# First feed-forward's way down in seven block products instead of eight, its weight sums on VectorE and one by an accumulating transfer; the second feed-forward's weight sums made later

## The chip, the cores and the metric

The kernel runs on one core of a Trainium2 chip. The metric is the device time of one execution in microseconds, first to last instruction with what lies around them; lower is better. Three executions of the kernel before took 1136.99, 1137.66 and 1139.56 us, median 1137.66.

## The reference, cut to what matters

One decoder layer runs on 576 token columns (512 of a prompt, 64 of samples) of 1024 channels. Two of its five sub-layers are feed-forwards of width 2816, called f1 and f2 below:

```
def swiglu(x, w_gate, w_up, w_down):
    return (jax.nn.silu(x @ w_gate) * (x @ w_up)) @ w_down
...
    x = x + 0.5 * swiglu(rmsnorm(x, p['ffn1_norm']), p['ffn1_w_gate'], p['ffn1_w_up'], p['ffn1_w_down'])
    h = rmsnorm(x, p['mix_norm'])
    proj = h @ p['w_in']
    ...
    x = x + jnp.concatenate([y_lru, y_pool], axis=-1) @ p['w_out']
    x = x + cross_attend(rmsnorm(x, p['xattn_norm']), mem_k, mem_v, p['xattn_wq'], p['xattn_wo'])
    x = x + 0.5 * swiglu(rmsnorm(x, p['ffn2_norm']), p['ffn2_w_gate'], p['ffn2_w_up'], p['ffn2_w_down'])
```

All values are float32. The way up of a feed-forward is `x @ w_gate` and `x @ w_up`; the way down is the last product with `w_down`.

## The kernel before, in words

Channels lie on the 128 partitions, tokens along the free axis, in two halves of 288 columns (`HT`). A float32 product is made of three fp32r products: every operand is split into a high part (a cast on ScalarE, tags ending in `h`) and a low part (a subtraction on VectorE, tags ending in `l`) by `split`, and high x high, high x low and low x high are summed in PSUM. One such trio on one 128x128 weight block and 288 columns is three matmuls; all large products are of this kind.

The 2816 hidden rows are 22 chunks of 128. The first 3 chunks of f1 (2 of f2) are plain products (`std`). For the rest, gate and up of a chunk form a 2x2 block matrix (gate/up by even/odd input channels) times a 2x2 block of the input (even/odd channels by token halves). `product` computes it with seven block products of 12 matmuls, named 11, E, F, G, 12, H and 22, where plain ones would be eight. The input's sums are made once; the weights' sums must be made for each chunk, and each weight block or sum is split. PSUM tiles of a chunk are `pu`, `pc` and `pa`. In program order a chunk f is 11, E, 22 of the chunk before, F, G, 12, H. After each of the seven stands one call of `fill()`, which takes steps of the way down from the queue `steps`, so that TensorE has work while VectorE and ScalarE prepare.

f2 (flag `fast`) also makes its way down in seven block products for 16 of its 22 chunks: hidden chunks 2p and 2p+1 are a pair, whose sums `build_a` and `build_b` make (tiles `ph`, `pl`); four chunks are a group g, and `quick(g)` puts 4 quads of output (one for two of the 8 output rows) of 6 steps each on the queue, 7 x 6 matmuls per quad. The weights of a quad are fetched into `td` (one buffer) and `t2`, and `ensure` sums and splits them into `dh`, `dl` (three buffers). The results go from PSUM through ScalarE (`take`) and an accumulating transfer on GpSimd's queue into `x`. The remaining six chunks are plain (`PLAIN`, `down`, PSUM tile `pd`).

f1 makes its whole way down plain: `down` over groups of 4, 4, 4, 5 and 5 chunks, 8 output rows each, 6 matmuls per chunk and row, spread by `fill` over the chunks. Its gate/up sums are three additions in VectorE (`prepare_a`) and one (`prepare_b`) on loaded blocks `r0`, `r1`.

Two of the weight sums of f2 (per gate/up chunk, and per quad of its way down) are made far ahead, in DRAM: `background` issues on GpSimd's queue a copy of weight blocks into the scratch tensors `gsum` and `dsum`, and two jobs later a transfer that adds a block to them. There are 36 jobs (20 and 16). Before, `background` is called in f1's chunks (29 times) and at the 12 input projections of the mixer (`proj`).

The order on TensorE within a feed-forward is the program's (`mm` chains the matmuls). On the other engines a scheduler sets the order when the kernel is built; each engine then runs its own list strictly in order. Weights pass through a ring of four 512 KB buffers (tag `wr`), loaded on SyncE's queue.

Of the kernel before, what the change touches and what calls it, by code (L numbers as in the profile page):

```python
# [16 lines left out]
P = 128  # L17
DC = 8
# [4 lines left out]
FGS = (4, 4, 4, 5, 5)  # L23
# [46 lines left out]
def hybrid_step(ctx, tc, a):  # L70
# [45 lines left out]
    neg = const.tile([P, 4 * DC], F32, name="neg")  # L116
    v.tensor_scalar(neg, cst[:, :4 * DC], -1.0, None, op0=ALU.mult)

    def ncol(name, i=0):
        c = _C[name] + i  # L120
        return neg[:, c:c + 1]


    s.activation(const.tile([P, 1], F32, name="table"), ones, AF.Silu)
# [248 lines left out]
    def ffn(name, n, fp, turn, plain, head=False, fast=False):  # L373
# [3 lines left out]
        wstd, wgu, wd = a[f"{name}_s"], a[f"{name}_gu"], a[f"{name}_d" + "p" * fast]  # L377
# [7 lines left out]
        def small_tile(nm_):  # L385
            return fp.tile([P, HT], F32, tag="pc", bufs=2 if fast else 3, name=nm_)

        def full_tile(nm_):
            return fp.tile([P, T], F32, tag="e", bufs=3 if fast else 2, name=nm_)
# [30 lines left out]
        def std_out(i, pg, pu):  # L420
# [4 lines left out]
            v.tensor_mul(e, e, half)  # L425
            for p, q in pieces(pu, e):
                v.scalar_tensor_tensor(out=q, in0=p, scalar=-1.0, in1=q, op0=ALU.mult, op1=ALU.mult)
            if fast:
                raw[i] = e
            else:  # L430
                split(hh[0][:, i, :], hl[0][:, i, :], e)
# [3 lines left out]

        def load(f):
            if f < FFC:
                raws[f] = [raw_tile(f"r{i}") for i in range(2)]
                for i in range(2):
                    nc.sync.dma_start(raws[f][i], wgu[f - plain, :, 2 * i:2 * i + 2])  # L440
# [6 lines left out]
        def prepare_a(f):  # L447
            if f >= FFC:
                return
            r0, r1 = raws[f]  # L450
            (w22, w11), (w12, w21) = ([t[:, i] for i in range(2)] for t in (r0, r1))
            w = W[f] = {}
            w["22"], w["11"] = parts_of(r0, "a")
            v.tensor_add(w22, w22, w21)
            v.tensor_add(w21, w21, w11)
            v.tensor_add(w11, w11, w22)  # L456
            w["E"], w["F"] = parts_of(r0, "e")

        def prepare_b(f):
            if f >= FFC:  # L460
                return
            r0, r1 = raws.pop(f)
            w = W[f]
            one = [fp.tile([P, KP, P], F32R, tag=tag, name=f"{tag}_b") for tag in ("oh", "ol")]
            split(*one, r1[:, 0])
            w["12"] = lambda q, k: one[q][:, k, :]
            v.tensor_add(r1[:, 0], r1[:, 0], r0[:, 1])  # L467
            w["G"], w["H"] = parts_of(r1, "g")


        def load_pairs(f):
            if f < FFC:
                w, e = wgu[f - plain], gsum[f - plain].rearrange("p b (k n) -> p b k n", n=P)
                raws[f] = [raw_tile(f"r{i}") for i in range(2)]
                for (i, b), src in zip(((0, 0), (0, 1), (1, 0), (1, 1)), (e[:, 0], w[:, 1], w[:, 2], e[:, 1])):
                    nc.sync.dma_start(raws[f][i][:, b], src)

        def load_22(f):
            if f < FFC:
                raw22[f] = wp.tile([P, KP, P], F32, tag="wr", bufs=WRB, name="r22")  # L480
                nc.sync.dma_start(raw22[f], wgu[f - plain, :, 0])
# [27 lines left out]
        groups = PLAIN if fast else [(sum(FGS[:i]), FGS[i]) for i in range(len(FGS))]  # L509
        panels = [(gi, j) for gi in range(len(groups)) for j in range(DC)]  # L510
        fetched, wdown = {}, {}

        def fetch(i):

            if i < len(panels) and i not in fetched:
                gi, j = panels[i]
                c0, fg = groups[gi]
                c0 -= PLAIN[0][0] * fast
# [16 lines left out]
        def down(gi, after=None):  # L535
# [4 lines left out]
            def step(j, k):  # L540
# [12 lines left out]
                elif k == fg - 1:  # L553
                    v.tensor_add(halves(x[:, j, :]), pd[j][:, :, :HT], halves(x[:, j, :]))
                    if after:
                        after(j)
# [1065 lines left out]
```

## Time and profile before

| | |
|---|---|
| runs | 1136.99, 1137.66, 1139.56 us |
| profiled execution | 1138.62 us, span 1136.7 us |
| mean granted TensorE clock | 0.996 |
| f1's seven-product chunks and its way down | about 50.8 to 401.8 us of the span |
| mixer, attention | about 401.8 to 742 us |
| f2 and the final norm | about 742 to 1136.7 us |

All times in the profile are microseconds from the start of the span unless marked ns. PE is TensorE (matmuls), PEld its weight loads, DVE VectorE, ACT ScalarE, POOL GpSimd, SP SyncE. A row of a group of instructions reads: source line, engine, operation, tiles written <- read, sizes, count, then busy time in us and mean ns of one, then the engine's idle time before them with what ended it. A row of the timeline reads: start, duration, engine, line, operation, and in brackets the idle time before it and what ended it. A row of a stretch gives the stretch's length, the busy time of each engine with its count, the granted clock, and the DMA engines' busy share and GB/s.

### The profile page before, as it was taken

How to read it: one execution, taken by the hardware profiler on the slowest of the kernel's cores; microseconds unless marked ns; L12 is line 12 of the kernel's file. 1: busy time of each engine (PE TensorE's matmuls, PEld its weight loads, DVE VectorE, ACT ScalarE, POOL GpSimd, SP SyncE). 2: the span in 40 equal slices, each digit the busy share in tenths (PEclk: the TensorE clock that was granted, in tenths of full speed). 3: DMA queues.
4: the chain of work that ended last, by engine and by line, in shares of the span. 5: the costliest groups of instructions: out<-in, count | busy, mean ns of one | idle time of the engine just before them, and what ended most of it. 6: DMA issues, size and time to landing. Idle time of an engine off the chain costs nothing.

```text
span 1136.7 us, 21329 instructions
## 1 busy us (share of the span) xinstructions
PE 1118.5 (98%) x8536; PEld 1101.0 (97%) x8536; DVE 832.0 (73%) x1387; ACT 610.9 (54%) x1052; POOL 134.4 (12%) x176
## 2 busy tenths in 40 slices
PE   8999999999999999999999999999999999999996
PEld 8999999999999999999999889999999999999996
DVE  8877778777775687986833566769878888787654
ACT  7644344344342454885622455546666666666554
POOL 0011111111111033310000000000121111212110
PEclk9999999999999999999999999999999999999998
DMA  8356766577674388642566762223675766766652
GB/s 293 117 146 152 185 167 149 140 162 188 155 182 107 103 236 191 119 141 94 174 217 215 261 229 92 66 89 93 162 176 148 182 172 160 188 167 154 148 115 84
DMA packets 82547, 179.58 MB, mean 158 GB/s; under 512 B 8272, under 2 KB 28752, under 8 KB 82320
## 3 DMA queue, kind: packets, MB, share of 16 engines
q1 hardware_dynamic: 55456, 129.66, 35.3%
q0 software_dynamic: 24064, 45.88, 22.9%
q10 hardware_dynamic: 2928, 2.67, 0.7%
q8 instruction: 67, 1.10, 0.4%
q14 instruction: 32, 0.26, 0.1%
HBM read 156.86 MB, written 34.17 MB: 168 GB/s over the span
## 4 chain that ended last, share of the span: by engine, by line
PE 91%; DVE 4%; ACT 2%; DMA 2%; issue 1%; DVEq 0%; SPq 0%; ACTq 0%
PE pu L136 23%; PE pd L136 15%; PE pc L136 11%; PE d L136 7%; PE pa L136 5%; PE q L136 5%; PE wo L136 5%; PE xo L136 5%; PE pg L136 3%; PE k L136 2%; PE v L1347 2%; PE in_l L136 2%; PE in_p L136 2%; PE o L136 1%; PE s L136 1%
## 5 line engine op out<-in xcount | busy, mean ns | idle before, releaser
L136 PE MATMUL pd<-hh,dl 128*128 128x288 f32 x352 | 75.3, 295 | 0.0
L136 PE MATMUL pd<-hh,dh 128*128 128x288 f32 x352 | 75.0, 294 | 0.0
L136 PE MATMUL pd<-hl,dh 128*128 128x288 f32 x352 | 75.0, 294 | 0.0
L178 ACT CAST wh_e<-r 128x1024 fp32r<-128x1024 f32 x39 | 41.0, 1051 | 57.1 <-DVE r L456 27.5
L136 PE MATMUL d<-ph,dh 128*128 128x288 f32 x224 | 66.8, 298 | 0.2 <-ACT add_e L659 0.2
L136 PE MATMUL d<-ph,dl 128*128 128x288 f32 x224 | 66.3, 296 | 0.0
L136 PE MATMUL d<-pl,dh 128*128 128x288 f32 x224 | 66.0, 295 | 0.0
L676 POOL DMA_DIRECT2D x<-add_e x16 | 19.3, 1204 | 380.9 <-ACT dh L178 348.6
L136 PEld LDWEIGHTS pd<-hh,dh 128*128 128x128 f32 x352 | 56.3, 188 | 0.0
L136 PEld LDWEIGHTS pd<-hh,dl 128*128 128x128 f32 x352 | 56.2, 188 | 0.0
L136 PEld LDWEIGHTS pd<-hl,dh 128*128 128x128 f32 x352 | 56.1, 188 | 0.0
L179 DVE TENSOR_TENSOR wl_e<-r,wh_e 128x1024 fp32r<-128x1024 f32 x39 | 47.7, 1222 | 11.1 <-ACT wh_e L178 11.1
L178 ACT CAST wh_g<-r 128x1024 fp32r<-128x1024 f32 x39 | 41.0, 1052 | 20.2 <-DVE r L467 14.4
L179 DVE TENSOR_TENSOR wl_g<-r,wh_g 128x1024 fp32r<-128x1024 f32 x39 | 47.7, 1222 | 5.2 <-ACT wh_g L178 4.1
L178 ACT CAST dh<-wr_d 128x512 fp32r<-128x512 f32 (+2 forms) x50 | 30.9, 619 | 34.5 <-PE pd L136 14.7
L136 PE MATMUL pu<-n1l,wh_a 128*128 128x288 f32 x152 | 44.9, 295 | 0.0
L136 PE MATMUL pu<-n1h,wl_a 128*128 128x288 f32 x152 | 44.8, 295 | 0.0
L136 PE MATMUL pu<-n1h,wh_a 128*128 128x288 f32 x152 | 44.7, 294 | 0.0
L907 ACT ACTIVATE g<-g 128x576 f32<-128x576 f32 x39 | 26.8, 686 | 32.2 <-DVE g L906 32.2
L136 PEld LDWEIGHTS d<-ph,dh 128*128 128x128 f32 x224 | 42.1, 188 | 0.8 <-ACT add_e L659 0.4
L136 PEld LDWEIGHTS d<-pl,dh 128*128 128x128 f32 x224 | 42.3, 189 | 0.0
L179 DVE TENSOR_TENSOR dl<-td,dh 128x512 fp32r<-128x512 f32 x48 | 33.1, 689 | 12.5 <-ACT dh L178 9.3
(561 smaller groups left out, 4235.3 us busy)
## 6 DMA issues: line engine op xcount, KB each, us to landing
gsum<-f_gu POOLq DMA_DIRECT2D x40, 512.0 KB, 8.6
r<-f_gu SPq DMA_DIRECT2D x38, 512.0 KB, 4.1
r<-f_gu SPq DMA_DIRECT2D x60, 256.0 KB, 4.1
x<-add POOLq DMA_DIRECT2D x40, 288.0 KB, 4.4
r<-gsum SPq DMA_DIRECT2D x40, 256.0 KB, 3.9
dsum<-f_d POOLq DMA_DIRECT2D x32, 256.0 KB, 5.7
ck<-ck SPq DMA_DIRECT2D x16, 512.0 KB, 4.4
cv<-cv SPq DMA_DIRECT2D x16, 512.0 KB, 7.2
```

The source lines that it names most:

```text
L136: i = te.matmul(*args, **kw)
L178: s.copy(hi, src)
L179: v.tensor_tensor(out=lo, in0=src, in1=f(hi), op=ALU.subtract)
L676: nc.gpsimd.dma_start(x[:, j:j + 2, HT:], t, accum_op=ALU.add)
L907: s.activation(g, g, AF.Silu, scale=-1.0)
L1347: te.matmul(ps[:, m, :HD], lhsT=lhs[:, kd, ms], rhs=w[wi][:, k, :], start=kd == 0 and i == 0, stop=kd == DC - 1 and i == 2)
```

## The change

- f1 uses the same scheme for its way down as f2: chunks 0 to 15 by `build_a`, `build_b`, `ensure` and `quick`, the last six plain.
- f1's weight sums can't be made ahead. Of the gate/up sums, `sum_eh` makes H = r0 + r0' on VectorE and E by a transfer on GpSimd's queue that adds a block from DRAM onto `r0` after H has been read; `sum_g` makes the other two on VectorE, as in f2. Of the sums of a quad of the way down, all four are made on VectorE (in f2, two of them come from `dsum`).
- f1's way down scales by 0.5 when it evicts (as f2 does), so `half` goes; the first 16 chunks and the plain group of two add into `x` by accumulating transfers, the last group of four on VectorE.
- `background` is called in f1's last five chunks, at the 8 last evictions of f1's way down, at the 12 projections of the mixer, at 6 of the 8 output projections and at the 8 of attention's output: 39 calls.
- In f1's head, the small products that spread the norm factor stand two weight blocks later (`mid`).
- In f2, `t2` is fetched with `td` and has two buffers.

```diff
         def load_pairs(f):
             if f < FFC:
-                ...
+                r0, r1 = raws[f] = [raw_tile(f"r{i}") for i in range(2)]
+                if head:
+                    nc.sync.dma_start(r0, w[:, 0:2])
+                    nc.sync.dma_start(r1[:, 0], w[:, 2])
+                else:
+                    ...
+        def sum_eh(f):
+            if f < FFC:
+                r0, r1 = raws[f]
+                v.tensor_add(r1[:, 1], r0[:, 0], r0[:, 1])
+                nc.gpsimd.dma_start(r0[:, 0], wgu[f - plain, :, 3], accum_op=ALU.add)
...
-                if k == fg - 1 and fast:
+                if k == fg - 1 and after:
+                    xj = halves(x[:, j, :])
+                    v.scalar_tensor_tensor(out=xj, in0=pd[j][:, :, :HT], scalar=0.5, in1=xj, op0=ALU.mult, op1=ALU.add)
+                    after(j)
+                    background()
+                elif k == fg - 1:
                     add = rows.tile([P, T], F32, tag="sq", name="add")
                     s.activation(halves(add), pd[j][:, :, :HT], AF.Copy, scale=0.5)
                     nc.gpsimd.dma_start(x[:, j, :], add, accum_op=ALU.add)
-                elif k == fg - 1:
-                    v.tensor_add(halves(x[:, j, :]), pd[j][:, :, :HT], halves(x[:, j, :]))
...
+                if head:
+                    nc.sync.dma_start(t[:, 0:3], wq[g, q, :, 0:3])
...
                     if k:
                         v.tensor_add(t[:, k], t[:, k], t[:, k - 1])
+                    elif head:
+                        v.tensor_add(t[:, 3], t[:, 0], t[:, 1])
+                        v.tensor_add(t[:, 0], t[:, 0], draw[i, 0])
                     split(*w, t[:, k:k + 2])
...
-        std(cols(ps1[1]), w, range(4))
+        mid = 6 if head else 4
+        std(cols(ps1[1]), w, range(mid))
...
         for f in range(plain, FFC):
             product(U, w["11"], n, N11, True)
...
             product(C, w["E"], n, T1, True)
...
             if before:
                 finish_chunk(before)
...
-                prepare_a(f + 1)
+            (sum_eh if head else prepare_e)(f + 1)
             fill()
...
             product(A, w["12"], n, N21, False)
...
+            if head:
+                prepare_e(f + 1)
...
             product(U, w["H"], n, T3, False)
...
+            if head:
+                sum_g(f + 1)
+                prepare_g(f + 1)
+                load_pairs(f + 2)
```

The first place is VectorE in f1's seven-product chunks. In the names, `wl_e`, `wl_g`, `wl_a` are low parts of weight sums of a gate/up chunk, `dl` of the way down's weights, L454 with an output `r1` in the kernel after is `sum_eh`'s addition, and `td` holds a quad's weights. Before, in a chunk of f1:

```order
L179 TENSOR_TENSOR wl_a_3662<-r0_3578,wh_a_3661 128x1024
L454 TENSOR_TENSOR r0_3578<-r0_3578,r1_3579 128x512
L455 TENSOR_TENSOR r1_3579<-r1_3579,r0_3578 128x512
L554 TENSOR_TENSOR x_66<-pd_3527,x_66 128x576
L179 TENSOR_TENSOR dl4_3634<-wr_d4_3525,dh4_3633 128x640
L456 TENSOR_TENSOR r0_3578<-r0_3578 128x512
L833 TENSOR_TENSOR g_3518<-pu_3409,g_3518 128x288
L179 TENSOR_TENSOR wl_e_3669<-r0_3578,wh_e_3668 128x1024
```

After, at the end of chunk 12 and the start of chunk 13. Between L454 and `wl_e_2872`, which reads the same `r0_2686` after the transfer has added to it, stand three instructions:

```order
L851 TENSOR_TENSOR e1_2552<-pu_2518,e1_2552 128x288
L610 TENSOR_TENSOR td9_2655<-td9_2655,t29_2657 128x256
L852 TENSOR_TENSOR g_2618<-e1_2552,g_2618 128x288
L454 TENSOR_TENSOR r1_2687<-r0_2686 128x512
L178 TENSOR_TENSOR dl90_2747<-td9_2655,dh90_2746 128x512
L178 TENSOR_TENSOR wl_22_2812<-r22_2538,wh_22_2811 128x512
L607 TENSOR_TENSOR td9_2655<-td9_2655 128x256
L178 TENSOR_TENSOR wl_e_2872<-r0_2686,wh_e_2871 128x1024
L178 TENSOR_TENSOR dl91_2784<-td9_2655,dh91_2783 128x512
```

The additions on `r0` in place have become one addition into `r1`, the transfer on another queue and two later additions; the way down's sums and splits stand among them. The second place is the same engine one chunk later: `dl102` is the last instruction on VectorE that reads `td10`, `td11` is loaded into the same single buffer, and L609 is the first that uses it.

```order
L178 TENSOR_TENSOR dl102_3052<-td10_2845,dh102_3051 128x512
L780 TENSOR_TENSOR g_2837<-pu_2698,g_2837 128x288
L470 TENSOR_TENSOR r0_2903<-r0_2903 128x512
L178 TENSOR_TENSOR dl103_3110<-t210_2847,dh103_3109 128x256
L471 TENSOR_TENSOR r0_2903<-r0_2903,r1_2904 128x512
L181 SCALAR_TENSOR_TENSOR pl6_2908<-g_2837,ph6_2907 128x576
L574 TENSOR_TENSOR g_2837<-g_2837,t2_2909 128x288
L609 TENSOR_TENSOR td11_3056<-td11_3056 128x256
```

Before, f1 had no `td`; its down weights went through the ring of four. The third place is GpSimd's queue from the end of f1 into the mixer (`u0`, `pe0` are the first buffers of the mixer's two branches; `gsum`, `dsum` are background transfers). Before:

```order
L165 DMA gsum13_110<-f2_gu 256x1x512
L168 DMA gsum14_111<-f2_gu 128x1024
L1093 MEMSET u0_4707 128x3
L1152 MEMSET pe0_4715 128x15
L1093 MEMSET u1_4780 128x3
L1094 COPY u0_4707<-st_4524 128x8x3
L1153 COPY pe0_4715<-st_4524 128x8x15
```

After:

```order
L164 DMA dsum1_119<-f2_d 256x1x256
L167 DMA dsum1_119<-f2_d 128x512
L164 DMA gsum5_103<-f2_gu 256x1x512
L167 DMA gsum6_104<-f2_gu 128x1024
L1027 MEMSET u0_5180 128x3
L1028 COPY u0_5180<-st_4997 128x8x3
L1086 MEMSET pe0_5188 128x15
L1087 COPY pe0_5188<-st_4997 128x8x15
```

Before, the last copy ahead of the mixer's first buffers is that into `gsum14`, the fifteenth of twenty; after, it is that into `gsum6`, the seventh, issued at the last eviction of f1.

More of the change, by code (lines that the diff above doesn't have):

```diff
@@ L424, in std_out @@
             s.activation(e, e, AF.Silu, scale=-1.0)
-            v.tensor_mul(e, e, half)
+            v.tensor_mul(e, e, r)
             for p, q in pieces(pu, e):
                 v.scalar_tensor_tensor(out=q, in0=p, scalar=-1.0, in1=q, op0=ALU.mult, op1=ALU.mult)
[L428 to L431, printed above, removed]
+            raw[i] = e
         raws, W = {}, {}
[L436 to L440, printed above, removed]
         def parts_of(src, nm_):
@@ L508, in ffn @@
         steps = deque()
-        groups = PLAIN if fast else [(sum(FGS[:i]), FGS[i]) for i in range(len(FGS))]
-        panels = [(gi, j) for gi in range(len(groups)) for j in range(DC)]
+        panels = [(gi, j) for gi in range(len(PLAIN)) for j in range(DC)]
         fetched, wdown = {}, {}
@@ L855, in ffn @@
             s.copy(A, U)
-            if fast:
+            if not (head and f == plain):
                 prepare_h(f)
-                load_22(f + 1)
-                if f == FFC - 5:
-                    fetch(0)
-            else:
+            load_22(f + 1)
+            if f == FFC - 5:
+                fetch(0)
+            if head and f >= FFC - 5:
                 background()
@@ L1268, in hybrid_step @@
                 mem_square(i)
+            background()
             if j == 5:
```

244 lines of the change are left out of this document (82 added, 162 removed).

## The prediction

> **What bounds the kernel now.** I read the page's busy times, the chain of work, the groups of instructions and then stretches.
>
> ```profile
> span 1136.7 us, 21329 instructions
> PE 1118.5 (98%) x8536; PEld 1101.0 (97%) x8536; DVE 832.0 (73%) x1387; ACT 610.9 (54%) x1052; POOL 134.4 (12%) x176
> PE 91%; DVE 4%; ACT 2%; DMA 2%; issue 1%; DVEq 0%; SPq 0%; ACTq 0%
> L136 PE MATMUL pd<-hh,dl 128*128 128x288 f32 x352 | 75.3, 295 | 0.0
> ```
>
> TensorE is busy for 98% of the span and carries 91% of the chain; `pd`, the plain way down, has no idle time ahead of it. So a matmul less is worth its step, as long as nothing else sets the pace. The step is read from a run of `pd` matmuls in the chain (start, us, what), and VectorE's load from stretches of f1 (first row) and of f2, which already runs the scheme that f1 gets (second); then f1's last evictions and the mixer.
>
> ```profile
> 367.56 34.38 PE pd L136 x258
> 100.00:200.00 100.00, 100.00 (x758) 100.00 (x757) 80.39 (x120) 42.34 (x65) 14.41 (x18) 1.00 0.67 163
> 800.00:900.00 100.00, 99.84 (x752) 99.47 (x751) 81.71 (x141) 66.95 (x136) 18.12 (x19) 1.00 0.69 167
> 382.00:390.00 8.00, 8.00 (x62) 8.00 (x61) 5.96 (x9) 4.17 (x7) 0.00 (x0) 1.00 0.33 98
> 414.00:422.00 8.00, 8.00 (x64) 8.00 (x63) 6.90 (x21) 2.58 (x3) 3.23 (x8) 1.00 0.96 241
> ```
>
> One matmul takes 34.38/258 = 0.133 us. At full clock TensorE has no gap in either feed-forward, and VectorE is 80 to 82% busy in both: f2's scheme fits when two of its sums per chunk and per quad come by transfer.
>
> **The removed products.** Plain, 16 chunks by 8 rows by 6 matmuls are 768; by sevenths, 16 quads of 42 are 672. 96 x 0.133 = 12.8 us off the path. Nothing else on TensorE changes in number.
>
> **The head.** The wait below is at the place where the norm's small matmuls now stand 12 matmuls (1.6 us) later.
>
> ```profile
> PE pg L136 <- DVE rf_n L272: 1.3, 1, 1.3
> ```
>
> It may go. But the order of VectorE puts `wl_e`, a sum of `td0` and one of `r0` (1.14 + 0.33 + 0.60 us by the rows below) ahead of the eviction that frees the next PSUM tile, about what is won. I take 0, between -1.3 and +1.
>
> **What VectorE gets.** From pc(8) to pc(12) of the new order, a group of four chunks, I count 12 instructions of 1024 columns, 28 of 512, 8 of 576, 38 of 288 and 20 of 256. These rows of f2 stand back to back, so that a start less the one before is the price:
>
> ```profile
> 889.94 0.41 DVE L639 TENSOR_TENSOR td<-td 128x256 f32<-128x256 f32 x1
> 890.27 0.45 DVE L915 TENSOR_TENSOR g<-e,g 128x288 f32<-128x288 f32 x1
> 890.64 1.22 DVE L179 TENSOR_TENSOR wl_e<-r,wh_e 128x1024 fp32r<-128x1024 f32 x1
> 891.78 0.45 DVE L596 TENSOR_TENSOR t<-g 128x288 f32<-128x288 f32 x1
> ...
> 893.49 0.69 DVE L492 TENSOR_TENSOR r<-r,r 128x512 f32<-128x512 f32 x1
> 894.09 0.75 DVE L179 TENSOR_TENSOR pl<-g,ph 128x576 fp32r<-128x576 f32 x1
> 894.76 0.69 DVE L179 TENSOR_TENSOR dl<-td,dh 128x512 fp32r<-128x512 f32 x1
> ...
> 896.03 0.42 DVE L639 TENSOR_TENSOR td<-td 128x256 f32<-128x256 f32 x1
> 897.14 0.69 DVE L179 TENSOR_TENSOR dl<-td,dh 128x512 fp32r<-128x512 f32 x1 [0.69 <-ACT dh L178]
> ```
>
> 256: 0.33, 288: 0.37, 512: 0.60, 576: 0.67, 1024: 1.14 us. Together 12 x 1.14 + 28 x 0.60 + 8 x 0.67 + 38 x 0.37 + 20 x 0.33 = 56.5 us. TensorE's group is 4 x 84 + 4 x 42 = 504 matmuls, 67.0 us. So 10.5 us are left for VectorE's waits, where f2 had 5.0 more (four sums of 512 and eight of 256 fewer: 2.4 + 2.6).
>
> Two kinds of wait don't shrink when VectorE is late, since each is released by VectorE itself. First, a sum, its cast on ScalarE and the subtraction: the last row waits 0.69 us so. In the order I find some six such places in a group where too little stands between, 3.5 us; f2 shows these as ScalarE's share of idle time:
>
> ```profile
> L179 DVE TENSOR_TENSOR dl<-td,dh 128x512 fp32r<-128x512 f32 x45 | 31.0, 689 | 11.8 <-ACT dh L178 8.6 <-PE pu L136 2.1
> L179 DVE TENSOR_TENSOR wl<-r,wh 128x512 fp32r<-128x512 f32 x15 | 10.3, 689 | 7.6 <-ACT wh L178 7.6
> L908 DVE TENSOR_TENSOR g<-g,rstd_n 128x576 f32<-128x576 f32 x15 | 11.4, 758 | 8.6 <-ACT g L907 8.6
> ```
>
> Those three wait for ScalarE 24.8 us in 15 chunks, 6.6 a group, much of it with time to spare. I take 4, between 2 and 6.6.
>
> Second, new waits on transfers: `sum_eh` (L454), transfer, cast, `wl_e`; and the last read of a `td`, its load, the next sum. No row shows an accumulate from DRAM into SBUF. The nearest (in the page's list of transfers, the last number is the us to landing):
>
> ```profile
> x<-add POOLq DMA_DIRECT2D x40, 288.0 KB, 4.4
> x<-add_e POOLq DMA_DIRECT2D x16, 288.0 KB, 6.4
> gsum<-f_gu POOLq DMA_DIRECT2D x40, 512.0 KB, 8.6
> r<-f_gu SPq DMA_DIRECT2D x60, 256.0 KB, 4.1
> td<-f_d SPq DMA_DIRECT2D x16, 256.0 KB, 5.0
> wr_o<-w_out SPq DMA_DIRECT2D x8, 512.0 KB, 3.6
> ```
>
> The cast takes 1.05 us:
>
> ```profile
> L178 ACT CAST wh_e<-r 128x1024 fp32r<-128x1024 f32 x15 | 15.8, 1053 | 5.4 <-PE pu L136 5.4
> ```
>
> I take 3.9 us for the accumulate: `x<-add` is nearest by queue, size and shape, and the evictions of the way down alone land from 3.5 us up (below), with f1's background gone. Ends: 3.5 and 6.4. With the cast and 0.3 for semaphores that is 5.3 us from L454's end to `wl_e`. In the order 6.7, 1.5, 8.6 and 3.9 us of VectorE's work stand between in the four chunks, so it waits 3.8 and, with the 0.7 of a cast counted above, 0.7 us. For a `td` load I take 4.2 us (384 KB in one piece; ends 3.6 and 5.0); 5.5, 4.4, 2.9 and 1.8 us of work and waits stand between, so it waits 0, 0, 1.4 and 2.5. Together 8.4 us.
>
> Landing of the evictions' transfer `add_1` alone (min, median, max):
>
> ```profile
> DMA to landing us min/median/max: 3.5/3.5/4.9
> ```
>
> The Trainium skill (DMA: Bandwidth & Descriptors, "Anatomy of one DMA — SWDGE (gpsimd) path") gives a transfer on GpSimd's queue 2.0 us plus its bytes at 436 GB/s, 2.6 us here; by that the longest accumulate wait loses 1.3 us a group, some 4 in all, and the sum would be 1129.7 (the other only passes its 0.7 on to the `td` behind it). The row above, 3.5 at the least on that queue, speaks against it.
>
> So VectorE's own loop is 56.5 + 4 + 8.4 = 68.9 us for a group of 67.0, +1.9. Three groups (chunks 4 to 15) are full; in chunks 16 to 21 the pair sums go and it catches up. The first group has shorter distances (3.1, 2.8, 6.0, 3.9), some 2 us worse. VectorE enters it about 1.7 us late, since chunk 3 has 9.6 us of products and 23 of VectorE work, and TensorE bears about 4 us of lateness before its nearest operand, the T1 sums of a pair, is late. That gives 3 x 1.9 + 2 + 1.7 - 4 = 5.4. ScalarE, 67% busy and in order, will now and then hand over later than its own time says: I add 0.8 a group, 2.4 in all. **Term: +7.8, from 0 to 24** (the upper end with the accumulate at 6.4 and `td` at 5.0: by the same distances 10.4 + 3.4 us of waits, a loop of 74.3).
>
> **What GpSimd and the transfers get.** Each background call is two transfers. At f1's end eight calls come in 8 x 24 x 0.133 = 25.5 us; before, this stretch had a DMA share of 0.33 and the mixer 0.96 without a gap on TensorE. The software queue's 45.88 MB took 22.9% of the span, 5.7 us of all engines per MB, so eight calls of 0.79 MB ask for 36 us. They stretch into the mixer, where VectorE needs the buffers that GpSimd clears by 418.1 and TensorE the gates at 430.2:
>
> ```profile
> q0 software_dynamic: 24064, 45.88, 22.9%
> 402.00 0.10 POOL L1093 MEMSET u<- 128x3 f32 x1 [38.79 <-PE pd L136]
> 418.10 0.46 DVE L1058 TENSOR_TENSOR u<-in_l,rstd_nm 128x288 f32<-128x288 f32 x1
> 430.18 1.63 PE pg L136 x12
> ```
>
> Copies of a kind follow at landing time (8.6 us for two calls of 3.2), so GpSimd gets there some 8 us late of the 16 it has. SyncE's first `w_in` panel shares the engines in the same stretch. I take +1, from 0 (covered) to +8 (8 us late against a cover of none). VectorE's evictions there, 2.7 us per row of 3.2, still fit. In the output projections and attention's output the calls hide behind panels loaded three ahead, and f2 only fetches `t2` earlier: 0.
>
> **The sum.** The profiled execution took 1138.62 us, 0.96 above the median of 1137.66. 1138.62 - 12.8 + 0 + 7.8 + 1 = 1134.6; against the median, 1133.6. I forecast 1133.6.
>
> **Rivals.** *VectorE keeps up.* If a group's waits stay under 10.5 us (accumulate at 3.5, `td` at 3.6, casts 3), the cover of 4 us lasts and the full 12.8 come: 1125. f2's idle time ahead of `wl_e` and `dl`, mostly with TensorE waiting for nothing, speaks for it; the 1.5 us between L454 and `wl_e` against.
>
> *The loop through the transfers sets the pace* (the other side). Accumulates that land after 5.4 us, midway between `x<-add` and `x<-add_e`, and `td` after 4.8 give waits of 5.3 + 2.2 + 0.4 + 1.9 + 1.5 = 11.3 us by the same distances, a loop of 71.8, and by the sum above 3 x 4.8 + 2 + 1.7 - 4 + 2.4 = 16.5: 1142.3. It decides from a loop of about 70.2 us on, where with the +1 above the 12.8 are paid back. The 6.4 of `x<-add_e` speaks for it; that its pieces are half as long as the accumulate's (288 columns against 512), against.
>
> *The accumulate's issue is held up behind VectorE.* If GpSimd can't issue it until an instruction of VectorE ends, the two short distances lose up to one 1024-wide instruction each, 2.3 us a group and 7 in all: 1140.6.
>
> ```profile
> L676 POOL DMA_DIRECT2D x<-add_e x16 | 19.3, 1204 | 380.9 <-ACT dh L178 348.6
> ```
>
> These issues take 1.2 us each beside a VectorE at 82%, and whether some of that is such a wait the row doesn't tell. The Trainium skill (SBUF — State Buffer, "SBUF: two separate sides") has such a mechanism: the two engines share a port under an exclusive lock, and descriptors of GpSimd's queue can starve behind VectorE.
>
> *The background calls clog f1's end.* 8 us instead of 1: 1140.6. For it: 36 us of transfers for 25.5; against: the mixer's 0.96.
>
> **The chances.** A part paid back, 1129 to 1138: 0.45. Full gain, 1123 to 1129: 0.22. The transfer loop: 0.20. The issue held up: 0.05. Clogging: 0.08. What a measurement of this kernel can tell from no change is about 0.2%, 2.3 us: below 1135.4 is faster, above 1139.9 slower. Faster: 0.22 + 0.34 = 0.56; same: 0.11 + 0.05 + 0.02 + 0.03 = 0.21; slower: 0.15 + 0.03 + 0.05 = 0.23. The range 1124 to 1144 leaves out the fastest end of the full gain and the upper half of the loop.
>
> **What would show it.** Right: 96 matmuls fewer; VectorE about 90% busy between 100 and 340 us, idle ahead of `wl_e` for ScalarE's cast behind the transfer and ahead of L609 for `td`; gaps of TensorE before `d` and `pu` in chunks 5 to 16 that add up to 5 to 10 us, none in 17 to 21. Wrong: no gap there (full gain), gaps of over 13 us (loop), accumulates in f1 that land far from 3.9 us, gaps at the first `in_l` or `pg` (clogging), or any in f2.

## The result, and the profile after

The kernel after takes 1184.97 us (median of four runs, 1180.79 to 1186.33), the kernel before 1138.45 (four runs, 1136.99 to 1139.56): ratio 1.0403, 95% interval 1.0373 to 1.0434. It is 46.5 us slower; the forecast was 1133.6, from 1124 to 1144. The profiled execution took 1185.88 us.

First the page of the kernel after: span, busy times, chain by engine, and TensorE's granted clock in 40 slices.

```profile
span 1184.1 us, 21744 instructions
PE 1132.3 (96%) x8440; PEld 1108.1 (94%) x8440; DVE 850.9 (72%) x1497; ACT 678.3 (57%) x1251; POOL 201.2 (17%) x251
PE 62%; issue 19%; DMA 7%; DVE 6%; POOL 3%; ACT 2%; SPq 0%; POOLq 0%; DVEq 0%; ACTq 0%
PEclk9998999999999898999999999999999999999998
```

The 96 matmuls are gone (8536 to 8440). Yet TensorE is busy 13.8 us longer (1132.3 for 1118.5) and idle 33.6 us longer (51.8 for 18.2). Since 12.8 us of work went, 26.6 us of busy time are new: 33.6 + 26.6 - 12.8 = 47.4, the difference of the spans. A matmul's end is modelled in the profile, so the edges of a gap count as busy too. From one matmul's start to the next, the waits cost some 40 us more than before and slow matmuls some 20 (in f1 about 30 and 10). The clock's row has an 8 in the slices from 89, 385 and 444 us, where before had 9s.

Where it went is read from the start of two stages, the mixer's first projection (`in_l`: matmul times in ns, min/median/max, then first and last start in us) and f2's first matmul (chain: start, us, what), two rows of before and two of after.

```profile
L136 PE MATMUL in_l<-nmh,wh_i x64: 292/294/380, 401.8 to 452.6; 128*128 128x288 f32 x64
742.08 6.39 PE pg L136 x48
L135 PE MATMUL in_l<-nmh,wh_i x64: 291/295/608, 430.6 to 496.1; 128*128 128x288 f32 x64
788.76 6.40 PE pg L135 x48
```

f1 ends 28.8 us later, though 12.8 shorter in work: it lost 41.6. Mixer and attention take 358.2 us for 340.3, +17.9 (the table further down counts to the very first matmul of f2, 0.2 us earlier in both). f2 takes 395.3 for 394.6, +0.7.

The stretches of the kernel after that answer to those shown of before (100 to 200 in f1, 800 to 900 in f2), and four of TensorE's longest waits (one of 5.5 us in the head, the same in both kernels, and one of 2.8 in the mixer are left out):

```profile
100.00:200.00 100.00, 95.85 (x708) 94.03 (x707) 83.24 (x151) 61.63 (x127) 22.22 (x23) 1.00 0.67 150
800.00:900.00 100.00, 100.00 (x760) 99.97 (x759) 81.10 (x142) 63.85 (x119) 10.23 (x10) 1.00 0.54 139
PE d L135 <- ACT d L638: 7.2, 5, 4.3
PE d L135 <- ACT add L630: 7.1, 8, 1.1
PE pu L135 <- DVE e L851: 6.1, 2, 5.9
PE d L135 <- ACT add_e L630: 2.7, 3, 1.1
```

In f1 TensorE waits for ScalarE's evictions of `d` (`add`, `add_e`, the copy L638), not directly for VectorE's sums. VectorE is 83% busy here and 81% between 100 and 340 us, not 90. One such wait in the group of chunks from 212 to 283 us, over GpSimd, ScalarE, VectorE and TensorE in the timeline (start, us, ..., idle before and its end):

```profile
232.31 0.94 POOL L455 DMA_DIRECT2D r<-f_gu  x1 [3.78 <-DMA x<-add_e]
236.90 1.05 ACT L177 CAST wh_e<-r 128x1024 fp32r<-128x1024 f32 x1 [3.71 <-DMA r<-f_gu]
237.98 1.23 DVE L178 TENSOR_TENSOR wl_e<-r,wh_e 128x1024 fp32r<-128x1024 f32 x1 [4.54 <-ACT wh_e L177]
238.14 0.41 ACT L630 ACTIVATE add<-d 128x288 f32<-128x288 f32 x1
238.61 0.40 PE L135 MATMUL d<-ph,dh 128*128 128x288 f32 x1 [1.11 <-ACT add L630]
```

The cast of `wh_e` waits for the E transfer issued at 232.3. ScalarE works in order, so the eviction `add` behind it runs only at 238.14, and TensorE waits for its PSUM tile. ScalarE waits so at 6 of f1's 19 casts of `wh_e`, 23.4 us in all: three times before 100 us, then once in each group of four chunks. The wait for `td` acts in the same way. At 205.97 us VectorE's first sum of a quad (L609) has waited 2.95 us for its load, ScalarE's cast of `wh_g` then waits 2.78 us for a sum behind it, and the evictions behind that cast come late: a gap of 0.71 us that ends at 211.96.

Behind some of the gaps the matmuls run slowly:

```profile
283.15 0.40 PE L135 MATMUL d<-ph,dh 128*128 128x288 f32 x1 [0.93 <-ACT add L630]
284.91 0.40 PE L135 MATMUL d<-ph,dh 128*128 128x288 f32 x1 [0.70 <-ACT add L630]
...
285.59 0.44 PE L135 MATMUL d<-ph,dh 128*128 128x288 f32 x1
285.83 0.44 PE L135 MATMUL d<-pl,dh 128*128 128x288 f32 x1
...
288.66 0.30 PE L135 MATMUL pu<-n1l,wh_h 128*128 128x288 f32 x1
288.80 0.30 PE L135 MATMUL pu<-n1h,wl_h 128*128 128x288 f32 x1
```

From 285.3 to 288.5 us a matmul takes 0.24 us, then 0.133 again. Other gaps are followed by no slow matmul, the like pair of 0.96 and 0.70 us that ends at 140.34 among them; the last section shows what tells them apart.

The second place is the end of f1. Chain, ScalarE and TensorE of the kernel after:

```profile
386.23 10.37 DMA x<-add
396.70 0.65 ACT L533 ACTIVATE add<-pd 128x576 f32<-128x576 f32 x1 [5.53 <-DMA x<-add]
399.00 0.61 PE L135 MATMUL pu<-n1h,wh 128*128 128x288 f32 x1 [5.88 <-DVE e L851]
382.00:390.00 8.00, 8.00 (x63) 8.00 (x62) 3.26 (x7) 3.08 (x6) 2.51 (x3) 1.00 0.99 199
```

With background calls in f1's last chunks the DMA engines are 99% busy here (0.33 before). An eviction's transfer lands after 10.4 us; the next eviction waits for its buffer (tag `sq`, two of them), the weights' cast stands behind it on ScalarE, their subtraction and VectorE's `e` behind that, and TensorE stops for 5.9 us. Then GpSimd:

```profile
407.79 1.06 POOL L164 DMA_DIRECT2D dsum<-f_d  x1 [2.06 <-PE pd L135]
413.54 1.07 POOL L164 DMA_DIRECT2D gsum<-f_gu  x1 [4.13 <-PE pd L135]
421.57 1.05 POOL L164 DMA_DIRECT2D dsum<-f_d  x1 [6.42 <-issue]
...
462.03 1.07 POOL L164 DMA_DIRECT2D gsum<-f_gu  x1 [4.58 <-issue]
463.13 0.62 POOL L1027 MEMSET u<- 128x3 f32 x1
469.40 0.80 PE L135 MATMUL pg<-uch,gwh 128*128 128x300 f32 x2 [2.84 <-ACT uch L177]
```

The eight calls of f1's last evictions leave from 407.8 to 462.0, one in 5.8 to 11.8 us. The mixer's first buffers, cleared behind them at 402.0 before, are cleared at 463.1, and the gates (`pg`, last row) come 39 us later than before.

### The profile page after: what moved, and what is told of

Same layout as the page of the kernel before. It is cut to its first block, busy times and chain, and to the rows that moved or that the text cites. A ratio compares the mean times of both kernels' runs of the same rounds, so it can differ in the third digit from the quotient of the medians.

```text
span 1184.1 us, 21744 instructions
## 1 busy us (share of the span) xinstructions
PE 1132.3 (96%) x8440; PEld 1108.1 (94%) x8440; DVE 850.9 (72%) x1497; ACT 678.3 (57%) x1251; POOL 201.2 (17%) x251
## 3 DMA queue, kind: packets, MB, share of 16 engines
q1 hardware_dynamic: 59344, 129.66, 33.6%
## 4 chain that ended last, share of the span: by engine, by line
PE 62%; issue 19%; DMA 7%; DVE 6%; POOL 3%; ACT 2%; SPq 0%; POOLq 0%; DVEq 0%; ACTq 0%
PE pu L135 12%; PE d L135 9%; PE pc L135 6%; PE pd L135 5%; PE q L135 4%; PE wo L135 4%; PE xo L135 4%; PE pa L135 3%; DMA x<-add_e 2%; PE pg L135 2%; PE v L1282 2%; PE k L135 2%; PE in_l L135 2%; PE in_p L135 1%; DMA x<-add 1%
## 5 line engine op out<-in xcount | busy, mean ns | idle before, releaser
L135 PE MATMUL d<-ph,dh 128*128 128x288 f32 x448 | 136.0, 303 | 17.2 <-ACT d L638 7.2
L135 PE MATMUL d<-pl,dh 128*128 128x288 f32 x448 | 133.1, 297 | 0.0
L135 PE MATMUL d<-ph,dl 128*128 128x288 f32 x448 | 133.0, 297 | 0.0
L135 PEld LDWEIGHTS d<-ph,dh 128*128 128x128 f32 x448 | 84.9, 189 | 22.6 <-ACT add L630 8.9
L135 PEld LDWEIGHTS d<-ph,dl 128*128 128x128 f32 x448 | 85.2, 190 | 0.0
L135 PEld LDWEIGHTS d<-pl,dh 128*128 128x128 f32 x448 | 85.0, 190 | 0.0
L177 ACT CAST dh<-td 128x512 fp32r<-128x512 f32 x96 | 59.3, 618 | 24.5 <-DVE td L607 20.8
L177 ACT CAST wh_e<-r 128x1024 fp32r<-128x1024 f32 x39 | 41.0, 1050 | 40.5 <-DMA r<-f_gu 23.4
L630 ACT ACTIVATE add<-d 128x288 f32<-128x288 f32 x128 | 51.4, 406 | 8.3 <-PE d L135 8.2
L178 DVE TENSOR_TENSOR wl_g<-r,wh_g 128x1024 fp32r<-128x1024 f32 x39 | 47.6, 1221 | 8.3 <-ACT wh_g L177 8.2
L177 ACT CAST wh_g<-r 128x1024 fp32r<-128x1024 f32 x39 | 41.0, 1050 | 17.3 <-DVE r L471 11.8
L177 ACT CAST wh_h<-r 128x1024 fp32r<-128x1024 f32 x39 | 40.9, 1050 | 16.1 <-PE pc L135 16.1
L178 DVE TENSOR_TENSOR wl_h<-r,wh_h 128x1024 fp32r<-128x1024 f32 x39 | 47.7, 1222 | 1.5 <-ACT wh_h L177 1.5
L455 POOL DMA_DIRECT2D r<-f_gu x19 | 17.9, 944 | 150.3 <-DVE r L454 40.9
```

Source lines behind the costliest of these rows:

```text
L135: i = te.matmul(*args, **kw)
L177: s.copy(hi, src)
L178: v.tensor_tensor(out=lo, in0=src, in1=f(hi), op=ALU.subtract)
L455: nc.gpsimd.dma_start(r0[:, 0], wgu[f - plain, :, 3], accum_op=ALU.add)
L630: s.activation(dst, src, AF.Copy, scale=0.5 * sign)
```

## The experiments

Theory 1: the wait for the E transfer costs f1 its time. Theory 2: the background transfers cost f1's end and the mixer theirs. Rivals: VectorE's amount of work and the `td` wait in f1; a late f1 in the mixer. "Start" is where the mixer's first `in_l` starts (end of f1) and "middle" the time from there to f2's first matmul, read in each run as above. They are of one profiled execution, which lies up to 5.5 us from the run's median (early_later, 1145.4), so small differences aren't read from them. Without any wait f1 would end at 401.8 - 12.8 = 389.0. The kernels whose names begin with `no_` leave out a part of the work and give other results; they only show what a part costs.

| kernel | median us | ratio to before (95%) | start | middle |
|---|---|---|---|---|
| before | 1136.4 to 1139.1 | 1 | 401.8 | 340.1 |
| after | 1184.97 | 1.0403 (1.0373-1.0434) | 430.6 | 358.0 |
| early | 1171.03 | 1.0301 (1.0286-1.0317) | 418.2 | 355.7 |
| no_e | 1157.63 | 1.0183 (1.0168-1.0199) | 405.5 | 355.1 |
| later | 1159.54 | 1.0204 (1.0179-1.0228) | 420.4 | 340.2 |
| early_later | 1150.94 | 1.0135 (1.0114-1.0157) | 407.7 | 340.3 |
| td_split | 1180.16 | 1.0375 (1.0345-1.0405) | 428.6 | 356.0 |
| all_three | 1156.47 | 1.0172 (1.0134-1.0210) | 414.1 | 340.3 |
| proj_kept | 1156.27 | 1.0164 (1.0138-1.0189) | 418.1 | 340.7 |
| f1_kept | 1180.64 | 1.0373 (1.0357-1.0389) | 431.3 | 353.8 |
| e_vec | 1160.86 | 1.0203 (1.0187-1.0219) | 409.0 | 355.0 |
| e_vec_proj | 1139.52 | 1.0012 (1.0003-1.0022) | 401.1 | 344.1 |
| e_vec_proj_td | 1138.36 | 1.0003 (0.9995-1.0012) | 399.8 | 340.3 |
| h_pool | 1155.97 | 1.0166 (1.0146-1.0186) | 415.5 | 341.8 |
| no_h | 1141.14 | 1.0037 (1.0020-1.0054) | 403.1 | 340.3 |
| no_f | 1137.64 | 0.9998 (0.9988-1.0007) | 399.6 | 340.7 |
| no_ta | 1133.18 | 0.9957 (0.9942-0.9972) | 394.6 | 342.5 |
| no_f_ta | 1131.45 | 0.9946 (0.9930-0.9963) | 392.0 | 341.5 |
| td_double | 1155.37 | 1.0148 (1.0134-1.0161) | 413.7 | 343.3 |
| ta2 | 1153.65 | 1.0121 (1.0101-1.0140) | 408.0 | 345.7 |

**The E transfer: early, no_e, e_vec.**

```diff
 early: in load_pairs, behind the load of r0
+    nc.gpsimd.dma_start(r0[:, 0], w[:, 3], accum_op=ALU.add)
+    nc.sync.dma_start(r1[:, 1], w[:, 0])
 and in sum_eh
-    v.tensor_add(r1[:, 1], r0[:, 0], r0[:, 1])
-    nc.gpsimd.dma_start(r0[:, 0], wgu[f - plain, :, 3], accum_op=ALU.add)
+    v.tensor_add(r1[:, 1], r1[:, 1], r0[:, 1])
 no_e: only sum_eh's transfer is left out
 e_vec: left out too, the first chunk's load_22 moved ahead, and in prepare_e, for f1
+    v.tensor_add(raws[f][0][:, 0], raws[f][0][:, 0], raw22[f])
```

> The kernel after, with f1's E sum taken off VectorE's line: the accumulating transfer follows the load of its block at once, and H is made in a second copy of that block (256 KB more to load for each of 19 chunks, 5 MB in all). Theory 1: f1 loses its time (31 us of TensorE's gaps and of slow steps behind them between 56 and 340 us) because the cast of wh_e on ScalarE waits for this transfer and holds up the PSUM evictions queued behind it. Then 20 to 30 us come back: 1155 to 1165 us, and ScalarE's idle time ahead of wh_e for the transfer is gone. Rival: VectorE's amount of work and the single td buffer set the pace; then under 8 us come back, 1177 or more. The mixer keeps its loss either way.

> The kernel after without f1's E transfers: the block is used unsummed, so the four products of f1's chunks that use E, G and F are of other numbers; all other instructions stay. It bounds what the transfer costs at its place. Theory 1: as much comes back as with the early transfer, or a few us more (no 5 MB more of loads, no 5 MB of accumulates): 1150 to 1163. Rival (VectorE's work, td): 1177 or more.

> The kernel after with f1's E sum made on VectorE (block d is already loaded for product 22, so no load is added; 19 accumulates of 256 KB and their waits go; VectorE gets 0.60 us more per chunk, 2.4 per group of four, 59 us of work). Theory 1 (the wait for the transfer, not VectorE's work, costs f1 its 31 us): nearly as much comes back as without the sum at all (1157.6): 1157 to 1162 us. Rival (VectorE's amount of work is what counts, as the prediction took it): more work on the engine that paces f1 makes it no better than with the early transfer: 1170 or more.

Without the transfer f1 ends 25.1 us earlier, and with the same sum on VectorE, though that is more work for it, 21.6 earlier: the transfer, and not the amount of work. The early transfer, which takes away the wait but keeps the transfer and adds 5 MB of loads, brings only 12.4, less than expected. So half of the gain is shown to be the wait as theory 1 has it; how much of the rest is the wait and how much the traffic of the 19 transfers was not told apart. The gaps of TensorE before 100 us are gone with the early transfer too, but a group of four chunks stays at 72 us. A group in stretches and VectorE's waits in it, in the kernel after (212 to 283 us), with the early transfer (211 to 283) and without one (195 to 264):

```profile
211.96:283.15 71.19, 67.63 (x499) 66.26 (x499) 56.71 (x105) 42.30 (x88) 15.64 (x16) 1.00 0.69 154
DVE wl_e L178 <- ACT wh_e L177: 7.3, 3, 4.5
DVE td L609 <- DMA td<-f_d: 4.0, 1, 4.0
...
210.64:282.97 72.33, 68.48 (x505) 67.01 (x505) 58.94 (x107) 43.61 (x90) 15.58 (x16) 1.00 0.72 166
DVE td L610 <- DMA td<-f_d: 6.3, 3, 2.6
DVE wl_e L178 <- ACT wh_e L177: 1.7, 3, 0.9
...
195.23:264.47 69.24, 67.61 (x505) 66.93 (x505) 58.53 (x107) 44.02 (x90) 12.05 (x12) 1.00 0.60 143
DVE wl_e L178 <- ACT wh_e L177: 4.9, 3, 2.2
DVE td L608 <- DMA td<-f_d: 2.6, 1, 2.6
```

VectorE's busy time (the fourth number, 56.7 to 58.9 us) is far below the stretch in all three. The early transfer takes 5.6 us from the wait for `wh_e`; longer waits for `td` (2.3 us), for the second copy of the block (1.4) and for `wh_g` (0.8) take most of its place.

**The background calls: later, proj_kept, f1_kept, early_later.** Calls taken out go to attention's projections.

```diff
 later: all three; proj_kept: the first two; f1_kept: the third
-            if head and f >= FFC - 5:
-                background()
-                    background()        # behind after(j) in down
-            background()                # behind project(ps[kind, c], ...) in proj
+            background()                # behind mem_k(j), query_out(j), in later also mem_v's panels
```

> The kernel after, with background called in no place of f1 and at none of the 12 input projections, but at the key, query and value projections of attention (8 calls each), at 6 output projections and at attention's output. Theory 2: the 24 us lost between 386 and 535 us come from the background transfers, which delay the eviction transfers of f1's plain group and the w_in panels; then 18 to 24 us come back, 1161 to 1167 us, with no gap over 1 us of TensorE there. Rival: the loss there is f1's own (its plain group evicts by transfers from ScalarE, its VectorE order is late); then under 6 us come back, 1179 or more. A second rival: the transfers are only moved, and attention loses what the mixer gains; then about 1185.

> The kernel after without background calls in f1's last five chunks and at its last evictions; the 12 at the input projections stay, the rest goes to attention. It tells two parts of the loss between 386 and 535 us apart. Theory 2a: the stall at 390 to 400 us (eviction transfers of f1's plain group queued behind background transfers, so that the next eviction waits for its buffer) goes, some 8 to 10 us with the slow steps behind it, while the input projections still lose: 1172 to 1178 us. Rival (the projections' calls are harmless alone, the queue was only full of f1's leftovers): the same as with all calls moved, 1157 to 1163.

> The other half: background calls stay in f1's last five chunks and at its last evictions, none at the input projections (moved to attention). Theory 2a: the stall at 390 to 400 us stays with its 8 to 10 us, and also part of the later ones, since the queue runs until about 425 us: 1165 to 1175 us. Rival (projections' calls carry it all): 1157 to 1163.

> Both edits (E sum's transfer at the load, background in attention). If the two losses are separate, the gains add: 1184 less 20 to 30 less 18 to 24, that is 1130 to 1146 us, by theory 1 and theory 2 about 1134. If one loss was the cause of the other, the sum falls short by 10 us or more.

Theory 2 holds, but my split of it fell: f1_kept came out slower than both of its ranges. Without f1's 13 calls the middle is back at 340.7 and f1 ends 12.5 us earlier, 30 together (28.7 in the medians). The 12 calls at the projections cost nothing by themselves, and taking out those alone brings 4.3 (f1_kept; its runs reach up to 1181.0, those of the kernel after down to 1180.8). In the run without f1's calls GpSimd clears the mixer's first buffer at 416.8, 1.3 us before its f1 ends:

```profile
416.78 0.10 POOL L1024 MEMSET u<- 128x3 f32 x1 [21.79 <-PE pd L135]
```

With both edits f1 ends at 407.7, and 34.0 us come back for 13.9 and 25.4 apart, 5.3 short of the sum: nearly two separate losses. The 1130 to 1146 forecast had counted on more from the early transfer.

**What is left in f1: e_vec_proj, td_split, all_three, e_vec_proj_td.** The first is e_vec with proj_kept; all_three is early_later with the cut and with H summed later; e_vec_proj_td is the first with the cut. td_split cuts f1's `td` in two and lets the third sum, and behind it the next quad's load, end the second piece (last two lines).

```diff
+    t = draw[i] = fp.tile([P, 2, 2, P], F32, tag="ta")        # a, b
+    c = draw[i, 1] = fp.tile([P, 2, 2, P], F32, tag="tc")     # c, a + b
...
+    v.tensor_add(c[:, 0], c[:, 0], t[:, 1])
+    fetch_pair(i + 1)
```

> The kernel after with the td buffer of f1 cut in two: a and b of a quad in one tile, c and the sum of a and b in another, and the third sum made one piece earlier, so that the load of the next quad's a and b starts one piece earlier (some 5 us). Nothing else changes. Theory: with the E transfer in its old place ScalarE's wait for it sets the pace of f1, and the td wait (4.0 us of VectorE's idle time in a group of four chunks, one group of 71.2 us) mostly lies beside it: 2 to 6 us come back, 1179 to 1183 us. Rival (the td wait carries f1's loss): 10 us or more, under 1175.

> E transfer at the load (H summed later, behind wl_e), td cut in two, background in attention. After the first two edits of the run before (1151 us) VectorE waited 6.3 us in a group for td, 1.4 for the second copy of the block; both should go. VectorE's group is then about 57 us of work and 4 to 5 of cast waits against TensorE's 67: f1's gaps vanish and the whole gain of 12.8 us appears: 1123 to 1128 us, the first version that beats the kernel before. Rival: another limit (ScalarE's order, the ring of wh buffers) keeps the group at 70 us or more: 1135 to 1150.

> E sum on VectorE, and no background calls in f1 (kept at the 12 input projections, the rest in attention). If the two gains add (27 less 2 and 29 us): 1185 - 25 - 29 = 1131 us, 1126 to 1136, the first version that beats the kernel before (1138). Rival: f1's group stays at 69 to 70 us, and TensorE's slow steps behind each gap with it: 1137 to 1143.

> The same with td cut in two. The kernel after gained 5 us by the cut alone (1180.2), and with the early transfer nothing (VectorE then waited 20.7 us in 240 for the tile's load, which stood behind 512 KB of gate/up blocks on SyncE's queue). Without the accumulates the transfers have more room: 2 to 5 us better than without the cut. Rival: the same queue makes it equal or up to 5 us worse.

The cut alone brings 4.8 us in the medians, as expected, though the runs overlap (1177.98 to 1184.10, and 1180.79 to 1186.33 without it). E on VectorE and no call in f1 come level with the kernel before (ratio 1.0012), in the rival's range: 12.1 us of f1's 12.8 are still lost. The cut there brings 1.2 us, less than the 2 to 5 expected. all_three is 5.5 us worse than early_later in the medians (the intervals of their ratios overlap), where 23 or more were to come back. VectorE's wait for the load did not go but grew, in all_three (first row, 100 to 340 us; 17.7 in early_later) and with E on VectorE (second, 90 to 340; 7.9 in e_vec_proj):

```profile
DVE tc L614 <- DMA ta<-f_d: 20.7, 8, 5.8
DVE tc L614 <- DMA ta<-f_d: 12.0, 6, 4.2
```

In all_three the load of `ta` is issued 0.7 us behind 512 KB of gate/up blocks on SyncE's queue (189.75 and 190.44 us), and the first sum starts 7.2 us after it.

**Work or load chain: h_pool, no_h, no_f, no_ta, no_f_ta**, all on e_vec_proj_td.

```diff
 h_pool -    v.tensor_add(r1[:, 1], r0[:, 0], r0[:, 1])
        +    nc.gpsimd.tensor_add(r1[:, 1], r0[:, 0], r0[:, 1])
 no_h   +    nc.sync.dma_start(r1[:, 1], wgu[f - plain, :, 1])
 no_f   -    v.tensor_add(r0[:, 0], r0[:, 1], r1[:, 0])        # f1 only
 no_ta  +    t = draw[i] = draw[0]                             # for i > 0, no load
```

> The version with E on VectorE, no background in f1 and td cut in two, with H (the sum of blocks a and b, needed only in the next chunk) made on GpSimd instead of VectorE: 19 additions of 512 columns. What is left of f1's loss there is a group of four chunks of about 69 us for TensorE's 67. Theory 3: the rest is VectorE's amount of work (59 us a group and some 9 us of waits); 4 x 0.60 = 2.4 us less work a group brings the group to 67 and 8 to 10 us back: 1128 to 1132, faster than both kernels. Rival: the rest is TensorE's waits for ScalarE's evictions, not work; then 0 to 2 us: 1136 to 1139. Second rival: GpSimd's additions slow VectorE or delay the eviction transfers behind them: 1140 or more.

> The same without the sum H: a block is loaded in its place (other numbers in two of f1's products), so VectorE has 2.4 us less work a group and GpSimd has no addition. Theory 3: 1128 to 1132, as with H on GpSimd; if it is much better than with H on GpSimd, GpSimd's addition has a price of its own. Rival: 1136 to 1139.

> The version with E on VectorE, no background in f1 and td cut in two (1138.4 us), without the last of f1's gate/up sums (F, L472): one addition of 512 columns less in each chunk, 2.4 us of VectorE a group, and no transfer more or less (one product of f1 gets other numbers). Theory 3, now clean of the extra load: if VectorE's amount of work paces what is left, the group falls from 69 towards 67 and 5 to 9 us come back: 1129 to 1133. Rival (theory 4: the chain of buffer released, load, sum, cast, subtraction paces it, and VectorE only waits longer): within 3 us of 1138.

> The same version with all sums, but f1's blocks a and b of the way down are loaded once and not for every quad (other numbers; 15 loads of 256 KB and VectorE's waits for them go, 12.0 us of its idle time between 90 and 340 us). Theory 4: the loads' chain paces what is left, 5 to 9 us come back: 1129 to 1133. Theory 3 (work): within 3 us of 1138.

> Both left out. If either alone already frees TensorE, no more is to be had than by the better of the two (floor: 1137.8 - 12.8 = 1125). If both are needed, this alone comes down to 1125 to 1130.

Theory 3 (VectorE's work) fell: an addition less per chunk changes nothing (no_f, 1137.64). no_h, which has an addition less but a load more, is 2.8 us slower, outside both its ranges: VectorE's wait ahead of E's sum (L465, 90 to 340 us) grows from 1.7 to 8.5 us. Without the load of `ta` 5.2 us come back, about half of what f1 still loses there (10.8 by its start), and with both left out 6.9; then TensorE has one gap over 0.3 us left in f1's loop (1.0), and f1 ends 3 us from its floor. So VectorE's waits for this load carry about half of the rest, and the addition counts, for some 2 us, only once they are gone. no_ta also moves less data; against that as the cause, the loads of `r` land after 3.6 us (median, 90 to 340 us) with and without it. That the single buffer is what makes the load late is theory 4's argument; the next runs were to show it and don't. The addition on GpSimd costs 17.6 us, as h_pool's second rival had it; the last section takes that up.

**A second buffer: td_double, ta2.**

```diff
-WRB, WSB = 4, 5
+WRB, WSB = 4, 4
+    w = [wp.tile([P, KP, P], F32R, tag=f"{tag}2", bufs=1) for tag in ("wh", "wl")]   # product 22
 td_double +  tag="td", bufs=2 if head else 1;  ta2 +  tag="ta", bufs=2
```

> E on VectorE, no background in f1, and td with two buffers (uncut), fetched a quad ahead; the 4 KB for it come from a buffer of their own for product 22's weights, which then leave four wh and wl buffers instead of five. No work is left out. Theory 4 (the chain of the single-buffered load paces the rest): as with the blocks loaded once (1133.2), 1131 to 1135 us, the first version faster than the kernel before (1138) beyond doubt. Rival: four wh buffers hold up ScalarE's casts, or attention's and the mixer's panels: 1137 or more.

> The same with td cut in two and only its first half (a and b) doubled. VectorE and ScalarE have one instruction more per quad than with td uncut. Theory 4: 1132 to 1136, at most 1.5 us behind the uncut version; rival: the half that is not doubled (c) still makes VectorE wait: 1136 or more.

Both miss, by 20 us and by 18, and come out in their rivals' ranges. VectorE now waits for gate/up blocks instead (H's, L454, 90 to 340 us of td_double and of ta2):

```profile
DVE r L454 <- DMA r<-f_gu: 12.4, 6, 3.0
DVE r L454 <- DMA r<-f_gu: 16.6, 9, 3.5
```

In td_double SyncE waits ahead of these loads (L443) until `wl_g` has been made from the buffer that they need, seven times in f1's loop and up to 11.8 us. Whether that comes from the new place of the quad's load on SyncE's queue or from the `wh` and `wl` buffers, four instead of five, stays open; the two edits were not made apart, so theory 4 is not settled by a kernel that keeps all the work. No version that keeps all the work is faster than the kernel before.

## Why the prediction was wrong, point by point

- *The removed products, -12.8:* right; 96 matmuls are gone, at 0.133 us each at full clock. *The head, 0, and f2, 0:* right. The wait for `rf_n` is gone and one for an eviction (`pg` for `e`, 1.1 us) stands in its place, as told; f2 took 0.7 us more.
- *"What GpSimd and the transfers get", +1 (0 to 8):* the worst step. f1's calls cost about 30 us (12.5 in f1, 17.3 behind it, by proj_kept). I sized the eight calls at f1's end by bandwidth (36 us), let GpSimd come 8 us late, and gave the five calls in f1's chunks no price; the trace has the eight leave over 55 us and the buffers cleared 61 us later than before. The mechanism of the clogging rival (1140.6) was right, its price a quarter. And I did not see that f1's own evictions now use the same queue, with two buffers: that is the stall of 5.9 us.
- *"What VectorE gets", +7.8 (0 to 24):* 41.6 less 12.5, some 29 us. Its work was right: 56.5 forecast, 56.7 measured in a group. The median landings were near: 4.4 us for the accumulate (3.9 taken), 3.4 for `td` (4.2 taken):

```profile
DMA to landing us min/median/max: 4.2/4.4/7.5
DMA to landing us min/median/max: 2.9/3.4/7.4
```

  VectorE's idle time in a group was 14.5 us where I had 12.4, and the group took 71.2 us, not 68.9: that is 7 us in three groups. The rest has two causes that the sum lacked. "TensorE bears about 4 us of lateness before its nearest operand" was false: the nearest thing is not an operand but a PSUM tile, whose eviction stands on ScalarE behind the cast that waits for the transfer. So before 100 us alone, where I had less than nothing, TensorE's three gaps take 8.2 us (2.29, 1.58 and 4.35) and the slow matmuls behind two of them about 4. Ahead of two of these gaps the accumulate landed after 6.0 and 7.5 us, longer than the 3.9 taken. And every gap was counted at its length only; slow matmuls add some 20 us in the whole kernel, about 10 of them in f1.
- *The rivals:* full gain and the issue held up fell; L455's issues on GpSimd took 0.9 us. The loop through the transfers came nearest in kind. But the condition given for it, landings of 5.4 and 4.8 us, was not met: it came with 4.4 and 3.4 in the median.
- *What would show it:* "gaps before `d`" was right, "5 to 10 us" and "VectorE about 90% busy" wrong. Those over 0.3 us between 90 and 340 us add up to 15.3, past the 13 named as the loop's sign, and those named for clogging came too: 2.4 us at `in_l` and 2.8 at `pg`.

## What to carry to other kernels

Ask of a new wait not only who needs the result but what stands behind the waiting instruction on an engine that works in order: here a cast held up PSUM evictions, and transfers held up the clearing of a later stage's buffers. Price a gap on TensorE above its length where the profile shows slow matmuls behind gaps, and look there whether several short gaps fall close together. A chain of buffer released, load, sum, cast, subtraction has a length that less work does not shorten, and taking out one wait of it shows the next: early_later, all_three, td_double and ta2 each met one.

## What the runs showed of the hardware

TensorE's matmul step was 0.24 us instead of 0.133 for about 3.2 us behind two gaps of 0.93 and 0.70 us (above), and from 95.1 to 100.6 us behind one of 4.35. In each run's trace the granted clock changes only at the edges of stretches of 3.41 us that follow each other without a break. These are four of them in the kernel after:

```profile
73.55:76.96 3.41, 1.99 (x15) 1.99 (x16) 2.89 (x5) 2.93 (x7) 0.00 (x0) 1.00 0.04 11
76.96:80.37 3.41, 3.41 (x28) 3.41 (x28) 3.41 (x9) 2.12 (x5) 1.22 (x1) 1.00 0.74 184
281.77:285.18 3.41, 1.77 (x12) 1.31 (x11) 2.36 (x4) 3.09 (x5) 0.00 (x0) 1.00 0.05 6
285.18:288.59 3.41, 3.41 (x16) 3.41 (x16) 3.33 (x7) 1.67 (x5) 0.70 (x2) 0.50 0.50 130
```

The gap of 1.58 us leaves TensorE idle for 42% of its stretch, and the next has the full clock. The two gaps of 0.93 and 0.70 fall into one stretch, together 48% of it, and the next has half the clock. The like pair before 140.34 falls into two stretches, idle for 23% and 25%. In f1 of all twenty kernels, each of the 20 changes to half the clock follows a stretch in which TensorE was idle for 48% or more; between 48% and 54% it also stayed, and below it always did. The Trainium skill ("TensorE: Matmul & The Clock Gate", "What's actually happening") has the clock halve after an idle window of about 3.4 us and come back after as long a busy one. The length of the window and the slower rate agree; here about half a window without work was enough.

GpSimd's additions slow VectorE. The first two rows are by shape, VectorE between 100 and 340 us, with the addition on GpSimd and with it on VectorE. The last two are from the timeline with it on GpSimd:

```profile
L178 DVE TENSOR_TENSOR wl_h<-r,wh_h 128x1024 fp32r<-128x1024 f32 x13 | 21.6, 1659 | 0.0
L178 DVE TENSOR_TENSOR wl_h<-r,wh_h 128x1024 fp32r<-128x1024 f32 x14 | 17.1, 1221 | 0.0
148.44 1.79 POOL L454 TENSOR_TENSOR r<-r 128x512 f32<-128x512 f32 x1
148.44 2.88 DVE L178 TENSOR_TENSOR wl_h<-r,wh_h 128x1024 fp32r<-128x1024 f32 x1
```

The subtraction of `wl_h` goes from 1221 to 1659 ns in the mean, a sum of `td` from 422 to 665. In the timeline the subtraction that starts together with an addition ends 1.09 us after it, close to its own 1.22. The Trainium skill ("SBUF — State Buffer", "SBUF: two separate sides") says that the two engines take a shared port by turns for whole instructions, and the trace agrees. The VectorE instructions beside the 16 additions from 63 to 334 us take 17.6 us more than the same shapes do in e_vec_proj_td, while the additions taken off it are only 16 x 0.60 = 9.6 us. How these 8 us more of VectorE's time become 17.6 us of the kernel's was not tried.
